# A two-layer encoder trunk: loads of the C values and of the bias rows put on GpSimd's queue, and a second buffer for loaded key rows

## The chip, the cores and the metric

The kernel runs on one core of one Trainium2 chip. The metric is the device time of one execution, in microseconds (us), smaller is better. A profiled execution has a span (first to last instruction) and a time of its own, which includes a little around the span.

## The reference, cut to what matters

The trunk has two layers over 2048 positions of width 1024, all in float32. In each layer a normalised input is projected into four groups of heads, each group does its own kind of attention, the four results are gated, concatenated, projected back and added to the input.

```python
for l in range(DEPTH):                                  # DEPTH = 2
    h = _rmsnorm(x, norm_g[l])
    z = jnp.einsum('bsd,de->bse', h, w_in[l])           # 1024 -> 3328 columns
    q_a, k_a, v_a, g_a, q_b, ..., g_d = jnp.split(z, offs, axis=-1)
    o_a = _dense_blocked(q_a, k_a, v_a, sc_hd)          # dense, 2048 keys for every query
    o_b = _window_sink(q_b, k_b, v_b, sink_b[l], sc_hd) # keys within 128 positions, sink logits
    o_c = _neighbourhood(q_c, k_c, v_c, rpb_c[l], sc_hd)
    o_d = _diff_blocked(q_d, k_d, v_d, lam, ...)        # difference of two softmaxes
    mix = concatenate([o_a * silu(g_a), o_b * silu(g_b), o_c * silu(g_c), o_d * silu(g_d)])
    x = x + jnp.einsum('bsm,md->bsd', mix, w_out[l])
return _rmsnorm(x, final_g)
```

Group C, which the change touches, sees the 2048 positions as a grid of 32 rows by 64 columns. Every query attends to a neighbourhood of 8 grid rows by 16 columns around it, and a learned bias by relative position is added to each logit:

```python
kg = jnp.take(k, idx, axis=1)...; vg = jnp.take(v, idx, axis=1)...   # 8 rows x 32 columns per block
sc = jnp.einsum('brcqhd,brclhd->brchql', qg, kg) * scale
sc = jnp.where(mask, sc + bias, NEG_INF)
p = jax.nn.softmax(sc, axis=-1)
o = jnp.einsum('brchql,brclhd->brcqhd', p, vg)
```

## The kernel before, in words

Each layer has three attention stages and an output projection. In the first stage the D columns of the input projection are computed for 16 tiles of 128 positions (`d_post`, `d_stack`). In the second, 32 units of D attention run while the rest of the input projection (A, B and C columns) is fed in between as filler; its results (q, k, v and gates of A, B and C) are stored to DRAM, the C values as `vc_d`, the C keys as `ksC`. The third stage, where the change lies, does the attention of A, B and C from those stored tensors. Then `out_proj` (L190) multiplies with `w_out`.

The third stage has two passes of 16 steps (the loop at L1117). In pass 0, step t does one unit of A (its first key head, 128 queries, 2048 keys) and two units of B. In pass 1, step t does one unit of A (second key head) and two units of C (two heads each); here a C tile is half of a band of 4 grid rows: `rg, ch = divmod(t, 2)`, band rg of eight, left or right half of the columns. One step issues scores on TensorE (S, Sb, Sc), max on VectorE (L497, L1001, L1037), exp on ScalarE, transposes of P (L513, L530) and their copies out of PSUM (L472, L474), and products with the values (L519 for A, L538 for B and C). At the end of a unit GpSimd multiplies the gate tile by the reciprocal of the softmax sum (`finish`, L543, tile gg, two buffers), TensorE transposes gg (`finish2`, L548), VectorE multiplies it with the output (L551, L558), and the product is stored to DRAM (mx, L552, L561).

What is loaded, and from where, in this stage:

- `k_batch` (L943): rows of stored keys (tile kl, 128 x 512 floats, pool "ql", L1068) come by a DMA of SyncE's queue (L947), are transposed on TensorE (kT, L98) and written into the key tiles. B and A need one kl for a batch, C two. Keys of C are made in pass 0, steps 12 to 15 (`prep`, L1098). Although the pool is named ql, only key rows live there; the queries (L963) have a pool of their own, qst.
- `load_vc` (L932): the values of C for a band, 9 or 12 grid rows by 40 columns for each half. Three grid rows of a half make one DMA (L940), 120 partitions of 1 KB, so 6 DMAs for the first and the last band and 8 for each other band, 60 in a layer. Destination is a slot of the pool "big" (10 slots).
- `load_bias` (L146): a tile of bias rows. GpSimd fills it with the mask value (L148), then four DMAs (L152), one for each grid row of the band, write 32 partitions by 4 heads by 320 floats each. The two inner tiles (bint, one for each half) serve bands 1 to 6; the tile of an edge band (bedge, one buffer, `cb`) is filled anew for each half of bands 0 and 7, so 6 bias tiles and 24 DMAs in a layer.
- `q_batch` (L959), `load_gate` (L608) and the stores of mx also issue from SyncE's queue.

The order of instructions on each queue is set by the framework when the kernel is built: the context is opened with `schedule_with_timeline_sim=True` (L1169). It plays the program through on a model of the engines and lets an instruction of later program order go ahead on its queue where the model finds the queue free and the operands and buffers ready. On the chip each queue then runs strictly in that fixed order, and an instruction that waits holds up all behind it. So a load written inside a C unit can stand many steps earlier on its queue, as soon as the model sees its buffer free.

Of the kernel before, what the change touches and what calls it, by code (L numbers as in the profile page):

```python
# [46 lines left out]
def c_window(rg):  # L47

    if rg == 0:
        return 0, 9  # L50
    if rg == 7:
        return 23, 9
    return 4 * rg - 4, 12
# [24 lines left out]
def trunk_kernel(ctx, tc, x, norm_g, w_in, w_out, qn_a, kn_a, sink_b, rpb_c, lam_q1, lam_k1, lam_q2, lam_k2,  # L78
                 subln_d, final_g, rope, bmask, out, depth=DEPTH):
    nc = tc.nc  # L80
# [65 lines left out]
    def load_bias(l, dst, rg, ch):  # L146
        w0, nr = c_window(rg)
        G.memset(dst, NEG)  # L148
        for r in range(4):
            i0 = min(max(4 * rg + r - 4, 0), 24) - w0  # L150
            row = w0 + i0 - 4 * rg - r + 7
            nc.sync.dma_start(out=dst[r * 32:r * 32 + 32, :, i0 * 40:i0 * 40 + 320],  # L152
                              in_=rep_d[l][ch][:, :, row * 40:row * 40 + 320])

    ht = {}
# [103 lines left out]
    for l in range(depth):  # L259
# [200 lines left out]
        with tc.tile_pool(name="sm", bufs=6, reuse_waits="tile") as sm, \  # L460
# [263 lines left out]
            with tc.tile_pool(name="st2", bufs=5, reuse_waits="tile") as st, tc.tile_pool(name="w2", bufs=10, reuse_waits="tile") as wp, \  # L724
# [175 lines left out]
                with tc.tile_pool(name="bb", bufs=1, reuse_waits="tile") as bbp, tc.tile_pool(name="p1", bufs=1, reuse_waits="tile") as p1p:  # L900
                    kds = {(0, 0): kd0[0], (0, 1): kd0[1]}

                    def get_kd(kv):
                        def f(c):
                            if (kv, c) not in kds:
# [7 lines left out]
                                  v=lambda h, j, kv=kv: vd[:, j, kv * 64:(kv + 1) * 64]) for kv in range(2) for t in range(NT)]  # L913
# [14 lines left out]
            def load_v(g):  # L928
                v = big2.tile([128, NT, 128], F32, tag="b", name=f"v{g}")
                nc.sync.dma_start(out=v, in_=vs_d[g])  # L930
                vt[g] = v

            def load_vc(rg):
                w0, nr = c_window(rg)
                v = big.tile([128, 2, 4, 256], F32, tag="b", name="vc")
                for ch in range(2):
                    for j in range(nr // 3):
                        k0 = (w0 + 3 * j) * 64 + 24 * ch
                        src = bass.AP(tensor=vc_d.tensor, offset=vc_d.offset + k0 * 256, ap=[[16384, 3], [256, 40], [1, 256]])
                        nc.sync.dma_start(out=v[0:120, ch, j, :], in_=src)  # L940
                return v

            def k_batch(ql, g, b):  # L943
                c = slice(b * 512, (b + 1) * 512)
                for pr in range(2 if g == "C" else 1):
                    kl = ql.tile([128, 4, 128], F32R, tag="kl", name="kl")
                    nc.sync.dma_start(out=kl.bitcast(F32), in_=ks_d[g, b][:, :, pr * 128:(pr + 1) * 128])  # L947
                    p = tps.tile([128, 512], F32, tag="t", name="kT")
                    for i in range(4):
                        transpose_raw(p[:, i * 128:(i + 1) * 128], kl[:, i, :])  # L950
                    if g != "A":
                        k0 = kt[g][2 * pr]
                        A.copy(k0[0:64, c], p[0:64, :])
                        V.tensor_tensor(k0[64:128, c], p[0:64, :], k0[0:64, c].bitcast(F32), op=ALU.subtract)
                    k1 = kt[g][2 * pr + 1]
                    A.copy(k1[64:128, c], p[64:128, :])
                    V.tensor_tensor(k1[0:64, c], p[64:128, :], k1[64:128, c].bitcast(F32), op=ALU.subtract)
# [94 lines left out]
            def a_unit(kv, t, q, pre):  # L1052
                return dict(kv=kv, t=t, s=a_scores, par=True, ev=EVA1 if kv else EV3, ns=8, nv=8, fin=fin_plain, fb=kv, q=q, pre=pre,
                            front=dense_front, back=dense_back, get_o=own_o, oc=0,
                            v=lambda h, j: vt["A"][:, j, kv * 64:(kv + 1) * 64])
# [8 lines left out]
            def small_unit(sc, i, t, q, px, fb, ns, nv, bias=None, pre=lambda: None):  # L1064
                return dict(kv=i, t=t, s=sc, par=False, ev=EVC if sc is c_scores else EVB, ns=ns, nv=nv, fin=fin_plain, fb=fb, q=q, pp=px, bias=bias, pre=pre,
                            front=small_front, back=small_back, get_o=pair_o, oc=128 * i, ptp=ptp)

            with tc.tile_pool(name="qst", bufs=2, reuse_waits="tile") as qst, tc.tile_pool(name="ql", bufs=1, reuse_waits="tile") as ql, \  # L1068
                    tc.tile_pool(name="cb", bufs=1, reuse_waits="tile") as cb, tc.tile_pool(name="px", bufs=4, reuse_waits="tile") as px, \
                    tc.tile_pool(name="pt", bufs=2, reuse_waits="tile") as ptp, \  # L1070
                    tc.tile_pool(name="ops2", bufs=1, space=PSUM, reuse_waits="tile") as ops2, \
                    tc.tile_pool(name="tps3", bufs=1, space=PSUM, reuse_waits="tile") as tps3:
                tpool = cycle([tps, tps, tps3])
                load_v("A")
                kt["B"] = [big.tile([128, S], F32R, tag="b", name=f"kB{i}") for i in range(2)]
                k_batch(ql, "B", 0)
                load_v("B")
                bint = [None, cb.tile([128, 4, 480], F32, name="bint1")]
                cc_ = {}
                cm = {"pool": cb}  # L1080
                qq = {}

                def prep(ps, t):
                    if t < NT:
                        g = "BC"[ps]
                        if ps == 0 and t % 4 == 2 and t < 14:
                            k_batch(ql, "B", t // 4 + 1)
                        if ps == 0 and t == 4:
                            kt["A"].append(big.tile([128, S], F32R, tag="b", name="kA1"))
                        if ps == 0 and 4 <= t < 8:  # L1090
                            k_batch(ql, "A", t - 4)
                        if ps == 1 and t == 2:
                            bint[0] = big2.tile([128, 4, 512], F32, tag="b", name="bint0")[:, :, 0:480]
                            load_bias(l, bint[0], 3, 0)
                        if ps == 0 and t == 8:
                            load_bias(l, bint[1], 3, 1)
                            kt["C"] = [big.tile([128, S], F32R, tag="b", name=f"kC{i}") for i in range(4)]
                        if ps == 0 and t >= 12:  # L1098
                            k_batch(ql, "C", t - 12)
                        qq["A", ps, t] = q_batch(qst, "A", t, 2 * ps, 2)  # L1100
                        qq[g, ps, t] = q_batch(qst, g, t, 0, 4)
                    elif ps == 0:
                        prep(1, 0)

                def get_bias(t, pr):
                    rg, ch = divmod(t, 2)
                    if ch == 0 and pr == 0:
                        cc_["v"] = load_vc(rg)
                    if rg not in (0, 7):
                        return bint[ch], cc_["v"]  # L1110
                    if pr == 0:
                        cc_["e"] = cb.tile([128, 4, 360], F32, tag="bedge", name="bedge")
                        load_bias(l, cc_["e"], rg, ch)
                    return cc_["e"], cc_["v"]
                prep(0, 0)
                units = []
                for ps in range(2):  # L1117
                    for t in range(NT):
                        units.append(a_unit(ps, t, lambda t=t, ps=ps: qq["A", ps, t], lambda t=t, ps=ps: prep(ps, t + 1)))
                        for i in range(2):  # L1120
                            if ps == 0:
                                units.append(small_unit(b_scores, i, t, lambda t=t: qq["B", 0, t], px, 2 + i, 2,
                                                        (min(t + 2, NT) - max(t - 1, 0) + 1) // 2))
                            else:
                                units.append(small_unit(c_scores, i, t, lambda t=t: qq["C", 1, t], px, 4 + i, 2, 2,
                                                        lambda t=t, i=i: get_bias(t, i)))
                                units[-1]["cm"] = cm
                def ex3(step):
                    if step == WOU:
                        for k in range(KD):  # L1130
                            if k == MS0:
                                ms_first.append(load_split(mx_d[0].rearrange("p a b -> p (a b)"), dv, "qd"))
                            wo_tiles.append(load_split(w_out[l, k * 128:(k + 1) * 128, :], dv, "qd"))
                drive([units[i:i + 3] for i in range(0, len(units), 3)], GAP3, iter(()), 0, ex3)
# [39 lines left out]
```

## Time and profile before

| what | value |
|---|---|
| median of 3 runs | 3717.33 us (3710.25 to 3719.14) |
| the profiled execution's own time | 3713.1 us |
| its span | 3711.3 us |
| mean granted TensorE clock in it | 0.978 of full speed |
| TensorE (PE) busy | 3516.1 us, 95% of the span |
| VectorE (DVE) busy | 2492.1 us, 67% |
| ScalarE (ACT) busy | 2095.2 us, 56% |
| GpSimd (POOL) busy | 944.4 us, 25% |
| third stage, about | 1081 to 1700 us (layer 0), 2945 to 3540 us (layer 1) |

Engines are named as in the profile: PE is the matmul side of TensorE, PEld its weight loads, DVE is VectorE, ACT ScalarE, POOL GpSimd, SP SyncE; SPq is SyncE's queue, whose rows are DMA issues. "L940" is line 940 of the kernel. In a timeline a row is: start, duration, engine, line, operation, output and inputs, count, and in brackets the idle time before it with the instruction that ended it. In a table of stretches a row is: the stretch, its length, then busy time (and count) of PE, PEld, DVE, ACT, POOL, then granted clock, DMA share and GB/s. In the list of waits a row is: who waited on whom, the total in us, how many times, the longest. In the chain of waits a row is: start, duration, and what the end of the program hung on at that time.

### The profile page before, as it was taken

Reading aid. Unit: us, or ns where it says so; the run is one execution under the profiler, and the core shown is the slowest. Engines: PE = TensorE matmul, PEld = TensorE weight load, DVE = VectorE, ACT = ScalarE, POOL = GpSimd, SP = SyncE. Lnnn points to the kernel's source line nnn. Section 1 sums busy time; section 2 is a strip of 40 time slices with the busy share of each in tenths; the row PEclk is TensorE's granted clock in tenths of the full one; section 3 lists DMA queues with packets and bytes.
Section 4 is the critical chain, followed back from the end, with each engine's and each line's share of the span. In section 5 each row is a group of like instructions: output and inputs, shape, how many; then the busy total and the mean of one; then the engine's idle time right before and its main releaser. Section 6 shows DMA issues by size and latency. Waiting matters only on the chain.

```text
span 3711.3 us, 71694 instructions
## 1 busy us (share of the span) xinstructions
PE 3516.1 (95%) x25232; PEld 2967.4 (80%) x25232; DVE 2492.1 (67%) x7829; ACT 2095.2 (56%) x3961; POOL 944.4 (25%) x1604
## 2 busy tenths in 40 slices
PE   8989999999989788999999899999999897899999
PEld 8979898888957666777899798989888676677787
DVE  4377878778777665774233778787877776667733
ACT  4345656556657565772143556565666676667721
POOL 4455324533100000001034553254321000000000
PEclk9999999999999998999999999999999899999999
DMA  4532225332133323325345323252232323343243
GB/s 142 191 100 83 80 76 172 86 83 83 59 98 86 89 83 107 93 78 181 132 129 192 98 78 86 78 182 73 78 84 73 90 81 92 88 117 89 87 151 119
DMA packets 353867, 386.44 MB, mean 104 GB/s; under 512 B 58914, under 2 KB 296674, under 8 KB 348386
## 3 DMA queue, kind: packets, MB, share of 16 engines
q1 hardware_dynamic: 349186, 366.11, 33.4%
q10 hardware_dynamic: 4320, 15.73, 1.2%
q8 instruction: 200, 3.28, 0.4%
q14 instruction: 161, 1.32, 0.1%
HBM read 258.83 MB, written 122.86 MB: 103 GB/s over the span
## 4 chain that ended last, share of the span: by engine, by line
PE 76%; DVE 7%; DMA 5%; POOL 4%; ACT 3%; issue 3%; SPq 2%; POOLq 0%; DVEq 0%; ACTq 0%
PE O L519 11%; PE S L496 10%; PE PTp L513 10%; PE y L222 10%; PE z L319 9%; PE z L321 9%; PE z L323 9%; DVE P L497 3%; PE PTp L530 2%; PE Obc L538 2%; ACT P L504 2%; PE Sc L1036 2%; SPq L940 1%; DMA wst<-in_w_in_dram 1%; DVE wt L313 1%
## 5 line engine op out<-in xcount | busy, mean ns | idle before, releaser
L497 DVE TENSOR_SCALAR_CACHE_REDUCE P<-S 128x512 f32<-128x512 f32 x1536 | 1017.7, 686 | 255.6 <-PE S L496 166.2
L319 PE MATMUL z<-wt,ht 128*128 128x256 f32 (+1 forms) x3008 | 891.3, 297 | 19.8 <-POOL wt L312 10.4
L321 PE MATMUL z<-wt,ht 128*128 128x256 f32 (+1 forms) x3008 | 882.9, 294 | 2.6 <-DVE wt L313 2.6
L323 PE MATMUL z<-wt,ht 128*128 128x256 f32 (+1 forms) x3008 | 882.3, 294 | 0.0
L513 PE MATMUL PTp<-idr,P 128*128 128x128 f32 x4096 | 624.6, 278 | 19.4 <-ACT P L474 10.3
L474 ACT COPY P<-PTp 128x512 f32<-128x512 f32 x864 | 491.3, 583 | 217.1 <-PE PTp L513 210.4
L319 PEld LDWEIGHTS z<-wt,ht 128*128 128x128 f32 x3008 | 568.8, 189 | 38.8 <-POOL wt L312 12.5
L504 ACT ACTIVATE P<-P,nm 128x2048 f32<-128x2048 f32 x256 | 513.9, 2008 | 144.4 <-DVE jk L503 139.9
L321 PEld LDWEIGHTS z<-wt,ht 128*128 128x128 f32 x3008 | 569.0, 189 | 16.1 <-DVE wt L313 4.6
L513 PEld LDWEIGHTS PTp<-idr,P 128*128 128x128 f32 x4096 | 491.5, 143 | 111.0 <-issue 23.6
L323 PEld LDWEIGHTS z<-wt,ht 128*128 128x128 f32 x3008 | 569.1, 189 | 8.4 <-issue 0.8
L496 PE MATMUL S<-kA,q 128*128 128x512 f32 x1024 | 348.1, 435 | 0.3
L543 POOL TENSOR_TENSOR gg<-gt,rzh 128x128 f32<-128x128 f32 x192 | 78.8, 411 | 1016.1 <-PE O L548 578.4
L222 PE MATMUL y<-wot,ms 128*128 128x512 f32 x1440 | 332.9, 393 | 3.4 <-ACT ms L211 2.0
L222 PEld LDWEIGHTS y<-wot,ms 128*128 128x128 f32 x1440 | 271.9, 189 | 64.2 <-ACT ms L211 2.4
L720 DVE SCALAR_TENSOR_TENSOR P<-P,cf,P 128x2048 f32<-128x2048 f32 x128 | 306.4, 2394 | 2.5
L312 POOL TENSOR_SCALAR wt<-wst,g 128x256 fp32r<-128x256 f32 (+1 forms) x336 | 208.2, 631 | 390.0 <-PE z L323 290.8
L504 ACT ACTIVATE P<-P,nm,rr_a 128x2048 f32<-128x2048 f32 x128 | 268.8, 2100 | 62.6 <-DVE jk L503 61.8
L519 PE MATMUL O<-P,vA 128*64 128x256 f32 x2048 | 272.6, 392 | 0.0
L519 PE MATMUL O<-P,vd 128*64 128x256 f32 x2048 | 240.9, 388 | 1.6 <-ACT P L474 1.6
L313 DVE SCALAR_TENSOR_TENSOR wt<-wst,g,wt 128x256 fp32r<-128x256 f32 (+1 forms) x344 | 195.3, 596 | 44.2 <-POOL wt L312 40.5
L496 PE MATMUL S<-kdt,qd 128*128 128x512 f32 x512 | 214.6, 442 | 8.3 <-DVE P L497 5.8
(195 smaller groups left out, 5130.6 us busy)
## 6 DMA issues: line engine op xcount, KB each, us to landing
wst<-in_w_in_dram SPq DMA_DIRECT2D x320, 128.0 KB
qd<-qd SPq DMA_DIRECT2D x128, 128.0 KB
htd<-ht SPq DMA_DIRECT2D x16, 1024.0 KB
ht<-htd SPq DMA_DIRECT2D x16, 1024.0 KB
q<-qsA SPq DMA_DIRECT2D x128, 128.0 KB
q<-qsB SPq DMA_DIRECT2D x64, 256.0 KB
q<-qc SPq DMA_DIRECT2D x64, 256.0 KB
mload<-mx ACTq DMA_DIRECT2D x30, 512.0 KB
```

What stands on the lines that cost most here:

```text
L222: PE.matmul(ys[c], lhsT=ms[:, a, kc], rhs=wts[k][:, b, c * 512:(c + 1) * 512], start=(k == 0 and i == 0), stop=(k == KD - 1 and i == 2))
L313: V.scalar_tensor_tensor(wt[:, 1, :], s, g8[:, k:k + 1], wt[:, 0, :].bitcast(F32), op0=ALU.mult, op1=ALU.subtract)
L319: PE.matmul(z, lhsT=h[:, 0, kc], rhs=wk[:, 0, :], start=(k == 0), stop=False)
L321: PE.matmul(z, lhsT=h[:, 0, kc], rhs=wk[:, 1, :], start=False, stop=False)
L323: PE.matmul(z, lhsT=h[:, 1, kc], rhs=wk[:, 0, :], start=False, stop=(k == KD - 1))
L474: A.copy(dst, src)
L496: PE.matmul(s, lhsT=q, rhs=k_ap[:, c:c + 512], start=(i == 0), stop=(i == len(q_list) - 1))
L497: V.tensor_scalar(p[:, c:c + 512], s, 1.0, None, op0=ALU.mult, op1=ALU.max, accum_out=mx[:, j:j + 1])
L504: A.activation(p, p, ACTF.Exp, bias=nm, scale=scale, accum_out=zacc)
L513: PE.transpose(tp[:, (h * 2 + a) * 128:(h * 2 + a + 1) * 128], p[:, h, j * 128:(j + 1) * 128], idn)
L519: PE.matmul(u["o"][a * 64:(a + 1) * 64, 0:256], lhsT=u["v"](0, j), rhs=u["p"][:, :, j * 128:(j + 1) * 128], start=(j >= NT - 2), stop=(j < 2))
L720: V.scalar_tensor_tensor(p0, p1, cf, p0, op0=ALU.mult, op1=ALU.add)
```

## The change

The 120 loads of C values (L940) and the 48 loads of bias rows (L152) are issued by GpSimd instead of SyncE, and the pool of the loaded key rows has two buffers instead of one. Nothing else is edited; the framework works out the order on all queues anew.

```diff
@@ load_bias @@
-            nc.sync.dma_start(out=dst[r * 32:r * 32 + 32, :, i0 * 40:i0 * 40 + 320],
+            nc.gpsimd.dma_start(out=dst[r * 32:r * 32 + 32, :, i0 * 40:i0 * 40 + 320],
                               in_=rep_d[l][ch][:, :, row * 40:row * 40 + 320])
@@ load_vc @@
-                        nc.sync.dma_start(out=v[0:120, ch, j, :], in_=src)
+                        nc.gpsimd.dma_start(out=v[0:120, ch, j, :], in_=src)
@@ the pools of the third stage @@
-            with tc.tile_pool(name="qst", bufs=2, reuse_waits="tile") as qst, tc.tile_pool(name="ql", bufs=1, reuse_waits="tile") as ql, \
+            with tc.tile_pool(name="qst", bufs=2, reuse_waits="tile") as qst, tc.tile_pool(name="ql", bufs=2, reuse_waits="tile") as ql, \
```

## The prediction

> **What bounds the kernel now.** I read the page first, then the chain of waits in the stretch where the page's PE slices dip, then the timelines of PE, SyncE's queue and GpSimd there.
>
> ```profile
> span 3711.3 us, 71694 instructions
> PE 3516.1 (95%) x25232; PEld 2967.4 (80%) x25232; DVE 2492.1 (67%) x7829; ACT 2095.2 (56%) x3961; POOL 944.4 (25%) x1604
> ```
>
> TensorE is busy 95% of the span, so all that a change of queues can win lies in the other 5%, 195 us, and in matmuls that run slowly after a pause. The edited lines belong to the third stage alone. There I cut the two layers into steps, from one transposed A gate (L548 into O) to the next: each row below is one step. The first and the fifth are undisturbed steps of pass 0 (with key rows of C) and of pass 1, the others are the long ones.
>
> ```profile
> 1261.68:1280.54 18.86, 17.96 (x141) 13.62 (x140) 15.13 (x55) 13.84 (x31) 1.20 (x3) 1.00 0.42 109
> 1280.54:1318.59 38.05, 19.57 (x136) 15.35 (x135) 15.41 (x54) 14.14 (x31) 1.20 (x3) 0.73 0.26 78
> 1372.03:1399.59 27.56, 18.62 (x118) 13.64 (x116) 12.46 (x39) 10.85 (x23) 4.14 (x5) 0.81 0.28 89
> 1399.59:1431.89 32.30, 18.70 (x127) 12.83 (x128) 11.73 (x47) 11.80 (x26) 2.49 (x4) 0.88 0.56 139
> 1484.83:1501.74 16.91, 16.91 (x142) 13.46 (x141) 12.44 (x46) 12.32 (x24) 1.20 (x3) 1.00 0.31 99
> 3126.47:3163.41 36.94, 18.82 (x136) 14.38 (x135) 15.33 (x54) 14.05 (x31) 1.20 (x3) 0.77 0.26 78
> 3216.56:3242.61 26.05, 17.93 (x118) 13.07 (x116) 12.10 (x39) 10.85 (x23) 4.16 (x5) 0.87 0.27 85
> 3242.61:3267.33 24.72, 18.66 (x128) 13.02 (x128) 12.79 (x46) 11.82 (x26) 2.49 (x4) 0.93 0.52 136
> ```
>
> An undisturbed step of pass 1 has PE busy for all of its 16.91 us: that is the floor, and moving loads cannot go under it. Six steps stand above their floor. Layer 0: 38.05 - 18.86 = 19.19, 27.56 - 16.91 = 10.65, 32.30 - 16.91 = 15.39. Layer 1: 36.94 - 18.86 = 18.08, 26.05 - 16.91 = 9.14, 24.72 - 16.91 = 7.81. The sum is **80.3 us**. It holds the pauses and the slow clock behind them (0.73 to 0.93 in those rows, 1.00 in the others). What PE waited for, layer 0 and then layer 1:
>
> ```profile
> PE kT L98 <- DMA kl<-ksC: 19.4, 3, 18.1
> PE Obc L538 <- DVE PT L472: 9.0, 2, 7.7
> PE O L548 <- ACT os L572: 8.5, 1, 8.5
> PE Sc L1036 <- DVE mxb L1037: 3.7, 1, 3.7
> ...
> PE kT L98 <- DMA kl<-ksC: 18.8, 3, 17.9
> PE Obc L538 <- DVE PT L472: 9.3, 2, 7.8
> PE Sc L1036 <- DVE mxb L1037: 4.4, 1, 4.4
> ```
>
> The first wait of each layer is the key rows of C. SyncE's queue says why: the load stood behind eleven loads of C values in a row. Its landing is in the chain of waits, and so is a later landing with nothing ahead of it.
>
> ```profile
> 1271.55 19.29 SPq L940 DMA_DIRECT2D vc<-vc  x11
> 1290.95 1.58 SPq L947 DMA_DIRECT2D kl<-ksC  x1
> ...
> 1290.95 8.41 DMA kl<-ksC
> ...
> 1316.89 3.00 DMA kl<-ksC
> ```
>
> The other waits come when pass 1 begins. VectorE and ScalarE stand still because a product could not be stored (mx), a bias tile had not come (bedge), and in layer 0 the next layer's sink logits (snk) were late. Each was issued between runs of C-value loads on the same queue, and each landed slowly:
>
> ```profile
> 1383.91 5.93 DMA mx<-mix
> ...
> 1401.11 10.69 DMA bedge<-rep
> ...
> 1422.85 6.16 DMA snk<-in_sink_b_dram
> ```
>
> **The change part by part: what leaves SyncE's queue.** Gone are 60 loads of C values and 24 of bias rows in each layer:
>
> ```profile
> L940 SPq DMA_DIRECT2D vc<-vc x120: 681/750/2484, 1266.4 to 3356.8; - x120
> L152 SPq DMA_DIRECT2D bedge<-rep x32: 538/597/1605, 1037.3 to 3493.9; - x32
> L152 SPq DMA_DIRECT2D bint<-rep x16: 538/568/634, 1033.8 to 3254.8; - x16
> ```
>
> By medians that is 60 x 0.75 + 16 x 0.60 + 8 x 0.57 = 59 us of queue time for a layer; in the long run it is 19.29 / 11 = 1.75 us a load. Of the two steps with 19.19 and 18.08 I count all but 1.5 us as gone: the key load is then issued at the end of the step's own short list, and the later landing of 3.00 us is what a single buffer still shows. The second key buffer works on the same stall from the other side, since a load may be issued while the tile before it is still being transposed; so either edit alone takes most of it, and together they earn it once. That is 37.3 - 1.5 = 35.8 us.
>
> Of the four steps at the start of pass 1 the excess is 10.65 + 15.39 + 9.14 + 7.81 = 43.0 us. Stores of mx, the sink logits, gates and queries stay on SyncE's queue and lose what stood before them. The bias tile does not: its fill and its four DMAs are now on one queue, GpSimd's.
>
> ```profile
> 1394.01 1.30 POOL L148 MEMSET bedge<- 128x1440 f32 x1 [16.16 <-DVE mxb L1037]
> ...
> 1399.52 4.03 SPq L152 DMA_DIRECT2D bedge<-rep  x4
> ```
>
> The fill waits until the tile's last reader is done; then 1.30 of fill, four issues and a landing must pass before the next half of the band can be scored. Before, that took 1411.8 - 1394.0 = 17.8 us; with four issues at 0.60 and a landing of 3 it is 1.3 + 2.4 + 3 = 6.7 us, less than a step, if no C-value load stands between. Some will, since 24 of a layer's 60 were issued between 1360.9 and 1421.4 us:
>
> ```profile
> L940 SPq DMA_DIRECT2D vc<-vc x24: 681/746/1754, 1360.9 to 1421.4; - x24
> ```
>
> I leave 4 us a layer for that, 8 in all, from bounds of 0 and of 11 (the tile no earlier than now, 17.8 - 6.7). That gives 43.0 - 8 = 35.0 us.
>
> **What GpSimd takes on.** The trace of before has no DMA issued from GpSimd, so the price of one there is unknown. The nearest rows are the same transfers from SyncE: 0.54 us below (a bias issue), 0.75 us (a C-value issue without a jam), 1.75 us above (in the jam). I take 0.75, the row of the same transfer; there is no reason for less than nothing. [...]
>
> Who waits behind such a load on GpSimd's queue? The gate products gg:
>
> ```profile
> 1485.18 0.40 POOL L543 TENSOR_TENSOR gg<-gt,rzh 128x128 f32<-128x128 f32 x1 [9.98 <-PE O L548]
> ...
> 1484.83 0.27 PE L548 MATMUL O<-idr,gg 128*128 128x128 f32 x1
> 1488.54 0.27 PE L548 MATMUL Obc<-idr,gg 128*128 128x128 f32 x1
> 1491.35 0.27 PE L548 MATMUL Obc<-idr,gg 128*128 128x128 f32 x1
> ```
>
> gg has two buffers: this one is written as soon as the transpose at 1484.83 frees its buffer, and transposed itself two transposes later, at 1491.35. So it may be late by 1491.35 - 1485.58 = 5.8 us before TensorE notices, and this is the tightest of the three in a step. A band's loads are 60 / 8 = 7.5 on average, 7.5 x 0.75 = 5.6 us if all stand in one piece ahead of it: within 5.8. GpSimd has the room too: 1.20 us busy in a step of 16.91. So the steady steps cost nothing at 0.75.
>
> At the start of the stage, eight bias loads are issued early and now fall between the last gates of D:
>
> ```profile
> 1033.81 2.56 SPq L152 DMA_DIRECT2D bint<-rep  x4
> ...
> 1037.31 2.48 SPq L152 DMA_DIRECT2D bedge<-rep  x4
> ...
> 1035.68 0.45 POOL L543 TENSOR_TENSOR gg<-gt,drs 128x128 f32<-128x128 f32 x1 [1.89 <-DVE drs L595]
> ```
>
> That gg ran as soon as its input drs came (1.89 us idle before it); a group of four loads of 2.5 us in front of it delays what follows by up to that, and there are two groups. I put 2 us for each layer, 4 in all, from 0 to 5.
>
> The sum: 35.8 + 35.0 - 4 = **66.8 us** less. The profiled execution took 3713.1 us, 1.8 more than its span; less 66.8 it would take 3646.3. The median of the three runs is 4.2 above the profiled one, so the forecast is 3717.3 - 66.8 = **3650.5 us**.
>
> **The rivals.** *The transfers stay in each other's way.* In the jam the loads went at 120 KB in 1.75 us, 69 GB/s, and the key rows landed 8.41 us after issue against 3.00. If that is a limit of the DMA engines and not of the queue, the late landings remain wherever they are issued from: 5.4 us for the key rows in each layer, 10.69 - 3 = 7.7 for bedge and 5.93 - 3 = 2.9 for mx in each, 6.16 - 3 = 3.2 for snk, in all 35.2; of the 80.3 there go 45.1, less the 1.5 and 4 of above: 39.6, which gives 3678. For it: the rate is flat through the run of eleven. Against: the DMA share is 0.26 in that step, so most engines had time. [...]
>
> *GpSimd's queue is the new wait (slower).* Place: gg behind a band's loads in the steady steps. If a load holds GpSimd for c us and each of the 16 bands' loads stands in one piece before the tight gg, TensorE loses 16 x (7.5c - 5.8). This eats the 66.8 at 7.5c = 10.0, c = 1.33 us. At the jammed 1.75 it is 16 x 7.3 = 117 us, so 50 slower: 3767. For it: nothing bounds c from above but the jam. Against: on SyncE the same burst was cut in two by short work, and five at 1.0 fit in 5.8.
>
> ```profile
> 1449.31 4.51 SPq L940 DMA_DIRECT2D vc<-vc  x5
> ...
> 1456.10 3.83 SPq L940 DMA_DIRECT2D vc<-vc  x3
> ```
>
> [...]
>
> *The place changes and the wait stays.* The order of all queues is worked out anew, and bias tiles behind C values on GpSimd could keep each bias tile 11 us late. With that (43.0 - 22 = 21), the D gates delayed by their 5 us a layer and c = 1.2 (16 x 3.2 = 51), the sum is 35.8 + 21 - 10 - 51 = -4: 3721, no change.
>
> **How the numbers follow.** The forecast's own case, with recoveries between 50 and 85, gets 0.62: the cause stands in the trace twice, in both layers, and the floor beside it. The transfers' rival gets 0.18, the place that changes 0.06, the slower one 0.14. A measurement of this kernel can tell about 0.3%, 11 us, from no change. Faster 0.80, the same 0.06, slower 0.14. The low end takes all 80.3 and the 7 us by which runs differ below the median: 3717 - 87 = 3630. The high end takes in the transfers' rival with the 8 us of bias left over and some of the spread: 3678 + 8 + 6 = 3692.
>
> **What would show it.** Right: the steps of 38.05 and 36.94 fall to about 19, those of 24.72 to 32.30 to 17 to 21, PE's wait for kl to under 4 us a layer, and the steady step stays at 16.91. The issue rows of vc on POOL show c; DMA landings of kl and bedge near 3 us speak against the transfers' rival, near 8 and 11 for it. Wrong: PE or PEld waiting for POOL gg, steady steps over 18, or a bias tile for band 0 that lands as late as now.

## The result, and the profile after

The changed kernel takes **3652.88 us** (median of 4 runs, 3651.88 to 3654.11); the kernel before, beside it, 3718.23 (3710.25 to 3726.55). The ratio is 0.9824, 95% interval 0.9802 to 0.9846. That is 65 us faster; the forecast was 3650.5, 67 us faster.

The profiled execution took 3653.0 us. The page of the changed kernel: TensorE is about as busy as before, GpSimd has 110 us more (the issues), the span is 60.0 us shorter.

```profile
span 3651.3 us, 71758 instructions
...
PE 3521.7 (96%) x25232; PEld 2959.9 (81%) x25232; DVE 2491.6 (68%) x7829; ACT 2094.8 (57%) x3961; POOL 1054.8 (29%) x1772
```

The same steps, cut in the same way (L548 to L548). In the table of stretches of the changed kernel the two key steps come first, then for each layer the four steps at the start of pass 1 as one stretch, then the four after them.

```profile
1290.65:1309.87 19.22, 18.34 (x136) 12.88 (x135) 15.13 (x54) 14.16 (x31) 1.20 (x3) 1.00 0.47 107
3094.84:3114.07 19.23, 18.35 (x137) 12.88 (x136) 15.13 (x54) 14.17 (x31) 1.20 (x3) 1.00 0.47 106
1348.41:1417.82 69.41, 65.45 (x488) 49.18 (x486) 47.11 (x181) 45.44 (x96) 32.35 (x51) 0.98 0.64 139
3152.61:3219.14 66.53, 64.62 (x487) 47.90 (x486) 45.91 (x180) 45.24 (x96) 32.64 (x52) 1.00 0.76 145
1417.82:1490.07 72.25, 72.25 (x556) 53.19 (x555) 50.39 (x179) 49.43 (x96) 16.76 (x30) 1.00 0.40 94
3219.14:3291.39 72.25, 72.25 (x555) 53.19 (x554) 50.39 (x179) 49.43 (x96) 16.14 (x30) 1.00 0.40 94
```

And the same two groups of four steps in the kernel before:

```profile
1357.60:1451.50 93.90, 71.36 (x487) 52.30 (x486) 48.68 (x181) 46.07 (x96) 9.03 (x15) 0.87 0.38 103
3202.16:3284.70 82.54, 68.36 (x487) 49.50 (x486) 48.71 (x180) 45.91 (x96) 9.05 (x15) 0.94 0.44 117
1451.50:1518.63 67.13, 67.13 (x556) 53.53 (x555) 49.30 (x180) 49.36 (x96) 4.80 (x12) 1.00 0.34 101
3284.70:3351.82 67.12, 67.12 (x555) 53.52 (x554) 49.29 (x179) 49.36 (x96) 4.80 (x12) 1.00 0.34 101
```

- Key steps: 38.05 to 19.22 and 36.94 to 19.23, **36.5 us** less.
- Start of pass 1: 93.90 to 69.41 and 82.54 to 66.53, **40.5 us** less. The clock is at 0.98 and 1.00 where it was 0.87 and 0.94: the pauses and the slow matmuls behind them went together.
- The next four steps: 67.13 to 72.25 and 67.12 to 72.25, **10.3 us** more, with TensorE busy all the time, at full clock, with the same number of matmuls. The forecast has no such term.
- All other steps of the stage: 3.1 less (the stage went from 578.5 to 538.7 and from 564.9 to 534.8 between its first and last gate). Ahead of the stage's first gate in layer 0: 11.1 us more, of which 5.4 lie in one interval of D's gates (below); the rest is spread over many intervals, and no run explains it. Between the two third stages 1.4 less, behind the second 0.1 more.

The sum, -36.5 - 40.5 + 10.3 - 3.1 + 11.1 - 1.4 + 0.1 = -60.0, is that of the spans.

In the list of waits of TensorE in layer 0's stage no wait for kl, for mx or for a bias tile is left among the large ones:

```profile
PE S L496 <- DVE P L497: 6.4, 7, 4.4
PE PTp L513 <- ACT P L474: 5.7, 5, 1.8
PE Obc L538 <- DVE ztb L1013: 4.0, 1, 4.0
```

The third of these comes from a late load that stayed: the sink logits, in the chain of the changed kernel, inside the one long step of layer 0 (24.76 us). It landed more slowly than before (6.16). In layer 1 a load of bias rows is in the chain:

```profile
1354.79 9.38 DMA snk<-in_sink_b_dram
...
3186.45 7.75 DMA bedge<-rep
```

The loads of bedge in the changed kernel, from issue to landing (us, min/median/max), lie between the 3 us and the 11 us that the prediction named as signs:

```profile
DMA to landing us min/median/max: 3.0/4.9/10.5
```

The price of an issue from GpSimd and the time to landing of the C values, from the rows of the tile vc in the changed kernel (ns for the issue, us to landing, each min/median/max):

```profile
L940 POOL DMA_DIRECT2D vc<-vc x120: 690/710/777, 1275.0 to 3294.2; - x120
...
DMA to landing us min/median/max: 4.8/6.4/12.4
```

A run of them holds GpSimd's queue no longer than that for each load, 6.34 / 9 = 0.70 us in its timeline, although they land slowly. Not all of them go out at once: 13 of the 120 issues stood behind the landing of an earlier load of C values, 11.1 us in all.

```profile
1275.03 6.34 POOL L940 DMA_DIRECT2D vc<-vc  x9
```

### The profile page after: what moved, and what is told of

It is laid out like the page before. It is cut to its first block, busy times and chain, and to the rows that moved or that the text cites. A ratio compares the mean times of both kernels' runs of the same rounds, so it can differ in the third digit from the quotient of the medians.

```text
span 3651.3 us, 71758 instructions
## 1 busy us (share of the span) xinstructions
PE 3521.7 (96%) x25232; PEld 2959.9 (81%) x25232; DVE 2491.6 (68%) x7829; ACT 2094.8 (57%) x3961; POOL 1054.8 (29%) x1772
## 4 chain that ended last, share of the span: by engine, by line
PE 70%; DVE 9%; POOL 3%; ACT 3%; issue 3%; DMA 3%; SPq 0%; POOLq 0%; DVEq 0%; ACTq 0%
PE O L519 11%; PE y L222 10%; PE S L496 9%; PE PTp L513 9%; PE z L319 7%; PE z L321 7%; PE z L323 7%; DVE P L497 4%; PE PTp L530 3%; PE Obc L538 3%; ACT P L504 2%; PE Sc L1036 2%; DVE wt L313 1%; DVE P L720 1%; POOL wt L312 1%
## 5 line engine op out<-in xcount | busy, mean ns | idle before, releaser
L319 PE MATMUL z<-wt,ht 128*128 128x256 f32 (+1 forms) x3008 | 892.1, 297 | 20.2 <-POOL wt L312 10.8
L519 PE MATMUL O<-P,vA 128*64 128x256 f32 x2048 | 278.5, 390 | 0.0
L519 PE MATMUL O<-P,vd 128*64 128x256 f32 x2048 | 242.8, 390 | 0.0
```

The source lines that it names most:

```text
L319: PE.matmul(z, lhsT=h[:, 0, kc], rhs=wk[:, 0, :], start=(k == 0), stop=False)
L519: PE.matmul(u["o"][a * 64:(a + 1) * 64, 0:256], lhsT=u["v"](0, j), rhs=u["p"][:, :, j * 128:(j + 1) * 128], start=(j >= NT - 2), stop=(j < 2))
```

## The experiments

Two theories stood against each other. **Queue**: SyncE's queue was too long, and taking 59 us of issues from it freed the loads behind. **Transfers**: the loads of C values themselves go slowly on the DMA engines, and the queue only showed it. Ratios are to the kernel before on the same chip, 3718 to 3724 us, each with its 95% interval.

**One part at a time.** Only the C values on GpSimd's queue:

```diff
-                        nc.sync.dma_start(out=v[0:120, ch, j, :], in_=src)
+                        nc.gpsimd.dma_start(out=v[0:120, ch, j, :], in_=src)
```

> Only the loads of C values go to GpSimd's queue; bias rows stay on SyncE's, one buffer for key rows. Queue theory (the stalls are time that SyncE's queue spends issuing C values): nearly the whole gain comes from this edit; both long key steps (38.05, 36.94) fall to 19 to 22 us, the four long steps at the start of pass 1 lose at least 35 of their 43 us of excess, time 3655 to 3668. Transfer theory (the C-value transfers hold the DMA engines wherever they are issued): the landings stay late, time about 3678. Buffer theory (the second key buffer earns the key steps): key steps stay above 30 us, time about 3690.

3662.72 us, 0.9838 (0.9824 to 0.9853). The key steps fall to 23.1 and 22.1 us; this part alone carries nearly all of the change. The steps of 18.3, 18.1, 17.5 and 18.3 after the start of pass 1 are here already.

TensorE's longest wait for kl in layer 0 falls from 18.1 to 4.0 us, though the load still lands slowly, in 6.36 us where it took 8.41. What changed more is that nothing stands ahead of it on SyncE's queue. So in the key steps the time on that queue was the larger part, and the slow landing the smaller. List of waits and chain of this kernel:

```profile
PE kT L98 <- DMA kl<-ksC: 5.2, 3, 4.0
...
1281.59 6.36 DMA kl<-ksC
```

Only the second buffer for key rows:

```diff
-... tc.tile_pool(name="ql", bufs=1, reuse_waits="tile") as ql, \
+... tc.tile_pool(name="ql", bufs=2, reuse_waits="tile") as ql, \
```

> Only the second buffer for key rows. Queue theory: the key load may be issued before the run of C values, so the key steps fall to about 19 and the start of pass 1 stays as long as before: 3718 - 36 = 3682. If the order still puts the load behind the run, nothing moves: 3718. Buffer theory: 3682, too, but then the kernel with both queue edits and one buffer keeps its long key steps.

3705.74 us, 0.9953 (0.9936 to 0.9970). The key steps are still 32.9 and 34.2 us. The wait for kl is gone from the list, and something else is late in its place:

```profile
PE PTp L530 <- DVE P L472: 13.0, 3, 12.2
```

The timeline of SyncE's queue in this kernel shows the run of eleven loads as it was, at 19.26 / 11 = 1.75 us each, ahead of key rows, gates and a store of mx:

```profile
1273.04 19.26 SPq L940 DMA_DIRECT2D vc<-vc  x11
1292.42 3.53 SPq L947 DMA_DIRECT2D kl<-ksC  x2
1296.37 1.04 SPq L616 DMA_DIRECT2D gt<-gsA  x1
1297.53 0.35 SPq L552 DMA_DIRECT2D mx<-mix  x1
```

So the second buffer cures one victim of the jam, not the jam.

C values and bias rows on GpSimd's queue, one key buffer (both `nc.gpsimd` edits of the diff above):

> Both queue edits, one buffer for key rows. Queue theory: the second buffer earns only the short waits for the second key tile of a batch, 0.6 us on PE and some more on what follows: 3653 to 3662, key steps 19 to 21 us. Buffer theory: key steps stay above 30, time about 3690.

3669.2 us, 0.9855 (0.9840 to 0.9870), beside 0.9838 for the C values alone: the bias rows add nothing.

C values on GpSimd's queue and two key buffers, bias rows left on SyncE's:

> C values on GpSimd's queue and two key buffers, bias rows back on SyncE's queue. Queue theory: the eight early bias loads no longer stand before the last D gates, which gives back the 5.4 us that layer 0 lost there, and SyncE's queue is free enough for the bias rows: 3645 to 3653. If the bias rows' place matters at the start of pass 1: above 3656, with bedge landing late again.

3647.83 us, 0.9793 (0.9777 to 0.9809): a little under the changed kernel's 0.9824. Moving the bias rows won nothing; if anything it cost.

**Does GpSimd's queue have slack?** The changed kernel with twice as many loads of C values, each with half of every row:

```diff
+                        for e in range(2):
...
+                            nc.gpsimd.dma_start(out=v[0:120, ch, j, 128 * e:128 * e + 128], in_=src)
```

> The changed kernel, but each load of C values is cut into two of half the floats (120 partitions of 512 bytes), so a band puts 16 issues on GpSimd's queue where it put 8. At the 0.70 us that an issue takes there a burst is 11.2 us. If a burst stands before a gate product that may be 5.8 us late, TensorE loses up to 5.4 us a band, 16 bands: up to 86 us, so up to 3739, and TensorE or its weight loads wait for POOL gg. If the gate products behind a burst have the 12 us that the first such step of the changed kernel shows: 3653 to 3660.

3651.25 us, 0.9813 (0.9798 to 0.9827): no slower, with 120 more issues at 0.72 us. In the third stage TensorE still waits for no gg. The slower rival lacked its price, and it lacked its place too.

**The late sink logits.** C values on GpSimd, two key buffers, and a tile of sink logits for each layer, so that they can be loaded early:

```diff
-        snk = lay.tile([128, 4], F32, tag="snk", name="snk")
+        snk = lay.tile([128, 4], F32, tag=f"snk{l}", name="snk")
```

> C values on GpSimd's queue, two key buffers, bias rows on SyncE's queue, and tiles of their own in each layer for the sink logits and their negatives, so that layer 1's load of them need not wait for layer 0's last reader. If that load, 9.4 us in landing with VectorE waiting for it, is what makes the step of 24.6 us in layer 0 longer than its twin of 19.2 in layer 1: 5 us less than with the one pair of tiles, about 3642. If VectorE would have waited for something else there: 3648.

3648.81 us, 0.9803 (0.9785 to 0.9822), not to be told from 3647.83. The step of 24.6 us is 19.2 now and the stage 4 us shorter in that trace, but it does not show in the time.

**Another queue.** The kernel of 3647.83 with the C values on ScalarE's queue instead of GpSimd's:

```diff
-                        nc.gpsimd.dma_start(out=v[0:120, ch, j, :], in_=src)
+                        nc.scalar.dma_start(out=v[0:120, ch, j, :], in_=src)
```

> Two key buffers, bias rows on SyncE's queue, and the C values issued from ScalarE's queue instead of GpSimd's. Queue theory: SyncE's queue is as free as with GpSimd, so the key steps fall to about 19, but ScalarE stands 0.75 to 1.75 us for each load between its exps and copies: 120 x 0.75 = 90 us of it, of which TensorE sees a part, 3660 to 3720. Transfer theory: runs of these loads take 1.75 us an issue there, too, and ScalarE is held up to 19 us at a time: above 3720.

3724.55 us, 1.0009 (1.0000 to 1.0019). SyncE's queue was relieved just as much, and in the key step of layer 0 TensorE waits for kl no more, yet all of the gain is gone. The jam went along with the loads: four in a row take 6.85 / 4 = 1.71 us each, ScalarE stands idle for 8 us behind them, and TensorE waits for ScalarE's copy. Timeline of ScalarE and list of TensorE's waits in this kernel:

```profile
1280.59 6.85 ACTq L940 DMA_DIRECT2D vc<-vc  x4
1287.48 0.37 ACT L474 COPY PT<-PTp 128x256 f32<-128x256 f32 x1 [8.01 <-issue]
...
PE Obc L538 <- ACT PT L474: 7.3, 1, 7.3
```

So the jam belongs to these loads and not to SyncE's queue. That a shorter SyncE queue is worth nothing does not follow, because here ScalarE's own work is held up in its place. The DMA view of that kernel in 1280:1288 us (queue, packets, MB, share of 16 engines) shows how the jam looks from the engines' side:

```profile
q10 hardware_dynamic: 533, 0.53, 20.2%
```

The kernel before in the middle of its jam, 1278:1290 us:

```profile
DMA packets 804, 0.82 MB, mean 68 GB/s; under 512 B 18, under 2 KB 803, under 8 KB 803
...
q1 hardware_dynamic: 803, 0.80, 20.2%
```

On both queues a fifth of the DMA engines' time and 67 to 68 GB/s, level. Three engines of 16 would be 18.75%. And three is the outermost count of the load's source, `[[16384, 3], [256, 40], [1, 256]]`: three grid rows of 40 positions. From GpSimd the same loads had a larger share of the engines. The changed kernel in 1274:1290 us, GpSimd's queue:

```profile
q0 software_dynamic: 2094, 1.42, 52.9%
```

The rate rose less than the share: 1.42 MB in 16 us is 89 GB/s.

That a load with three outer rows works on three engines only is the author's reading of these two shares, 20.2% and 20.2%; which engines they were the profile does not say. The next two kernels give the loads 40 and 120 outer rows.

**The shape, without any move.** The kernel before, each load of C values cut into its three grid rows of 40 positions, all on SyncE's queue, one key buffer:

```diff
-                        src = bass.AP(..., ap=[[16384, 3], [256, 40], [1, 256]])
-                        nc.sync.dma_start(out=v[0:120, ch, j, :], in_=src)
+                        for r in range(3):
+                            src = bass.AP(..., offset=... + (k0 + 64 * r) * 256, ap=[[256, 40], [1, 256]])
+                            nc.sync.dma_start(out=v[40 * r:40 * r + 40, ch, j, :], in_=src)
```

> The kernel before, but each load of C values is cut into three of one grid row each (40 partitions of 1 KB), all still on SyncE's queue: 180 issues in a layer instead of 60. Queue theory (what counts is the number of issues and their time on SyncE's queue): 180 issues of 0.3 to 0.5 us take 54 to 90 us of the queue instead of 45, so the key steps stay above 30 us and the time is 3718 or more. Transfer theory (a three-row load is confined to few DMA engines, which is what makes an issue take 1.75 us in a run): the jam goes, an issue in a run costs what a lone one does, eleven loads take 33 x 0.4 = 13 us instead of 19.3, key steps fall by 5 us or more each and the time to about 3695.

**3631.48 us**, 0.9759 (0.9742 to 0.9775): faster than the change by 0.0065 of the time, 24 us, with three times as many loads on the queue that was thought too long. SyncE's timeline: 18 short loads, six of the old ones, in 7.57 us, 1.26 for each old one, and the key load behind them.

```profile
1271.22 7.57 SPq L941 DMA_DIRECT2D vc<-vc  x18
1278.90 0.56 SPq L948 DMA_DIRECT2D kl<-ksC  x1
```

This left two readings, shape or size of a load. So the kernel before with one load as ever, 120 partitions of 1 KB, but from 120 successive positions:

```diff
-ap=[[16384, 3], [256, 40], [1, 256]]
+ap=[[256, 120], [1, 256]]
```

> The kernel before with one edit: a load of C values reads 120 successive positions instead of 40 positions from each of 3 grid rows. Bytes, partitions, queue (SyncE), number of loads and the order on TensorE, ScalarE and GpSimd are those of before; the values that come are others, so the output is not the reference's. If the jam is the shape of the load (three outer rows put it on few DMA engines, 120 KB in 1.75 us), it goes although nothing left the queue: the load issues in about 0.75 us in a long run, the key steps take 19 to 21 us, the time is 3625 to 3645 us, as with loads cut by grid rows (3631). If SyncE's queue itself is the limit (that many rows of 1 KB for one queue), the loads still take 1.75 us in a row, the steps stay at 37 to 38 us and the time at 3721.

This is an experiment and no kernel to use, since group C gets values of other positions.

3632.01 us, 0.9760 (0.9746 to 0.9773). Number, size and queue of the loads are those of before, and so is the order on ScalarE and GpSimd, and on TensorE but for a few swapped matmuls; only the shape differs. Here the 120 rows also follow each other without a gap in DRAM; the cut loads above read the same rows as before, with gaps, and won as much. **The cause of the jam is the shape.** The timeline of SyncE's queue, ten loads in a row at 0.48 us where eleven took 19.29:

```profile
1274.02 4.83 SPq L940 DMA_DIRECT2D vc<-vc  x10
```

The DMA view of the same kernel in 1274:1279 us shows a share five times the 20.2% of before:

```profile
q1 hardware_dynamic: 1216, 1.26, 100.8%
```

And in its chain the neighbours that had landed late, key rows (8.41 before), sink logits (6.16) and mx (5.93):

```profile
1281.76 3.46 DMA kl<-ksC
...
1366.27 3.08 DMA snk<-in_sink_b_dram
1374.62 3.02 DMA mx<-mix
```

**On top of the cut.** Cut loads on SyncE's queue, and two key buffers:

> The kernel before with each load of C values cut into three of 40 partitions, all on SyncE's queue, and two buffers for key rows. If the shape was the cause and is cured by the cut, the second buffer has left only the 1.4 and 0.9 us by which the key steps stand above 18.9, and the order of the queues is made anew: 3625 to 3635 us, the same as the cut alone. If it works as it did beside GpSimd's loads (3662.7 to 3647.8 us), 15 us go: 3617.

**3623.17 us**, 0.9741 (0.9728 to 0.9754), the fastest kernel of all here, 0.8% under the changed one. Its key steps are as short as the changed kernel's, and both groups of four steps at the start of pass 1 take 62.26 us (1339.12 to 1401.38 and 3131.03 to 3193.29), where the changed kernel has 69.41 and 66.53. Its table of stretches, the two key steps and two of the four steps at the start of pass 1:

```profile
1281.37:1300.61 19.24, 18.35 (x137) 12.90 (x136) 15.15 (x54) 14.18 (x31) 1.21 (x3) 1.00 0.48 133
3073.29:3092.52 19.23, 18.35 (x136) 12.89 (x135) 15.13 (x54) 14.16 (x31) 1.20 (x3) 1.00 0.46 131
1353.53:1368.28 14.75, 14.75 (x117) 11.69 (x116) 11.46 (x39) 11.32 (x23) 4.20 (x5) 1.00 0.51 137
1368.28:1384.71 16.43, 16.41 (x128) 12.46 (x127) 13.54 (x50) 11.77 (x25) 2.50 (x4) 1.00 0.71 171
```

The changed kernel with cut loads, on GpSimd's queue:

> The changed kernel with each load of C values cut into three of 40 partitions, on GpSimd's queue. If three outer rows slow the transfers there too, the landings of C values fall from 6.4 us (median) to about 3 to 4 and the late sink logits of layer 0 with them (the step of 24.8 us falls by 4 to 6), the 10 us of the new order and 5 of the gates of D stay: 3642 to 3648 us. If GpSimd's descriptors were spread over the engines anyway, landings stay near 6 and the time at 3652. If three short loads hold GpSimd longer than one (3 x 0.4 against 0.71 us) and gg comes late, 3655 to 3690.

3649.86 us, 0.9808 (0.9794 to 0.9821). The rows of vc: landings fall from 6.4 to 2.5 us (median), each with a third of the bytes. The last of three is issued 1.03 us after the first, so by these medians a whole old load is in after some 3.5 us (an estimate) against 6.4: the shape seems to slow them on GpSimd too. But three short loads hold its queue for 1.54 us where one took 0.71, and the time is the changed kernel's within the intervals.

```profile
L941 POOL DMA_DIRECT2D vc<-vc x360: 512/514/593, 1273.3 to 3305.2; - x180
...
DMA to landing us min/median/max: 1.8/2.5/5.4
```

The last kernel is the fastest one with the bias rows alone on GpSimd's queue:

> Against the version with cut loads of C values on SyncE's queue and two key buffers (0.9741 of before): the bias rows alone go to GpSimd's queue. If the two groups of four loads between the last gates of D cost what they did in the changed kernel (5.4 us in layer 0, nothing in layer 1) and a bias tile in pass 1 is as quick by either queue, 3628 us, ratio 0.9755. If the bias rows carry most of the 26 us between that version and the one with all these loads on GpSimd's queue, 3640 to 3649, ratio 0.979 to 0.981. If moving them costs nothing, 0.974.

Ratio 0.9772 (0.9758 to 0.9786) against 0.9741, that is 0.0031 x 3718 = 11.5 us slower. The same difference separates the changed kernel (0.9824) from the one with its bias rows on SyncE (0.9793), though there the intervals overlap. GpSimd's timeline just before layer 0's third stage shows the part that can be placed: between D's sums and the gate product stand eight issues, 4.59 us.

```profile
1033.89 0.70 POOL L118 TENSOR_TENSOR drs<-dme,epst 128x2 f32<-128x2 f32 x1 [2.15 <-DVE dme L116]
1034.53 2.41 POOL L152 DMA_DIRECT2D bint<-rep  x4
1036.93 2.18 POOL L152 DMA_DIRECT2D bedge<-rep  x4
1039.12 0.41 POOL L543 TENSOR_TENSOR gg<-gt,drs 128x128 f32<-128x128 f32 x1
```

The interval between the two D outputs there is 32.1 to 32.2 us in every kernel with bias rows on GpSimd, and 26.7 to 26.8 in the others. In layer 1 no interval grew so. Besides these 5.4 us, some 4 are in the two third stages (529.7 and 527.8 against 526.9 and 526.5), and the rest lies where no edited line is; what it comes from stays open.

## Why the prediction was right, point by point

- **Where the time was.** In six steps around the key loads and the start of pass 1: right. How much it was: too low, because the floor was. 16.91 us is a step with 142 matmuls, and the step of 27.56 that it was subtracted from has 118. In that place the fastest kernel has a step of 14.75 us, and its four steps at the start of pass 1 take 93.90 - 62.26 = 31.6 and 82.54 - 62.26 = 20.3 us less than before, where the prediction saw 43.0 in both layers together. Its gain, 0.0259 x 3718 = 96 us, is above the 80.3.
- **The key steps**, -35.8 forecast, -36.5 measured: right. But "either edit alone takes most of it" holds for the C values only (23.1 and 22.1 us); the second buffer alone left 32.9 and 34.2, because gates and a store of mx stood behind the same jam.
- **The start of pass 1**, -35.0 forecast, -40.5 measured. The low floor hid some of what could be won, and the 8 us left for late bias tiles were too much. What did stay is 7.1 and 4.3 us against the 62.26 of the fastest kernel. TensorE is idle for only 4.0 and 1.9 us of it (69.41 - 65.45 and 66.53 - 64.62); the 4.0 are the wait for the sink logits, so late bias tiles can have cost 1.9 at most. The rest is TensorE being busy for longer with the same matmuls. The steps one by one did not fall to 17 to 21 us as foreseen: work moved between them (24.76, 13.50, 13.00 and 18.16 in layer 0), so that only the groups of four can be compared.
- **The gates of D**, +4 forecast, 2 in each layer: +5.4 in layer 0, nothing to be seen in layer 1. Both groups of four issues came ahead of one gate, so they added up.
- **The price on GpSimd's queue**, 0.75 us taken, 0.71 measured, never above 0.78 in the changed kernel. The 1.0 and 1.2 that the rivals reckon with are assumed values that no run shows; five loads at 0.71 are 3.6 us. gg behind a whole band of loads was no wait of TensorE; the doubled loads confirm the slack.
- **"So the steady steps cost nothing": wrong in what it covers.** Two groups of four steps cost 10.3 us more, with three of the four over the 18 us that the prediction named as a sign of being wrong. gg is not the reason, since TensorE waits for nothing in them. The framework's new order is: in one such step of the changed kernel TensorE's half-width products (128*64, L519) stand in five pieces of 12, 4, 4, 6 and 6, before in two of 16. By the grouped lines of the first of these stretches, after and then before, the same 128 matmuls take 18.6 us instead of 15.6, which is 3.0 of the 5.1 us, and the other groups grow a little too:

```profile
L519 PE MATMUL O<-P,vA 128*64 128x256 f32 x128 | 18.6, 391 | 0.0
```

```profile
L519 PE MATMUL O<-P,vA 128*64 128x256 f32 x128 | 15.6, 385 | 0.0
```

  The longer steps came wherever whole loads of C values went to GpSimd (18.3, 18.1, 17.5 and 18.3 us also with the C values alone), and not with the flat loads, whose order on TensorE is nearly that of before (16.4, 16.9, 16.9 and 16.9). That the pieces are the reason is read from these rows; no run shows it by itself.
- **The sum**, -66.8 forecast, is -65.4 by the medians and -60.1 by the two profiled executions (3713.1 and 3653.0); the runs of before spread over 16 us. That it came so near is partly luck. The 10.3 of the longer steps were missed, and so were 7.1 ahead of layer 0's third stage, beyond the 4 that were counted. Against them stand 5.5 more at the start of pass 1, 0.7 in the key steps, 3.1 in other steps and 1.3 elsewhere, and the last 5 lie in the choice of before: its median, 3718.23, is that much above its profiled execution.
- **The reason was right as far as it went, and stopped short.** That the key load stood behind the run of C values is borne out: the wait for kl of 18.1 us ended with the landing at 1290.95 + 8.41 = 1299.4, so it began at 1281.3, and 9.7 us of it were over before the load was issued; with the C values on GpSimd as the only edit, the wait for kl in layer 0 fell by 14.1 us, to 4.0, and a faster landing (6.36 us against 8.41) gave only 2.1 of that. Why the run took 1.75 us a load was not asked. The argument against the transfers' rival was that the DMA share was 0.26, "so most engines had time". They had; the loads did not use them, and the level 68 GB/s went with a share of 20.2%, near the 18.75% of three engines (the author's estimate; no run counts them). With another shape on the same queue both halves of the stall go, the time on the queue and the slow landing (3.46 us). GpSimd's queue helps because a run of these loads holds it for 0.70 us each, where it holds SyncE's for 1.75 and ScalarE's for 1.71; how much the larger share of the engines adds no run separates. The rival had the cause right and the price wrong: it took the slow landings as costing the same wherever the loads are issued from. They stayed in part, for the C values (6.4 us), the sink logits (9.38), the bias rows (median 4.9) and, with one buffer, the key rows (6.36), but they cost TensorE little.
- **The time to issue** was not small here: eleven issues held SyncE's queue for 19.29 us, and from GpSimd the C values alone gave 0.9838. The ScalarE run (1.0009) moved the held time to another engine and saved none.

## What to carry to other kernels

When a run of equal loads on one queue goes at a level rate well below what the DMA engines move elsewhere, look at the shape of the load before its queue. Here, on one queue, three outermost entries went with 20.2% of the engines' time and 68 GB/s, 120 of them with 100.8% and 253 GB/s. Try a long count outermost, or cut the load; here that won 2.4% in a few edited lines, and the move to another queue, with a second buffer, 1.8%. A change of queues also makes the order on all engines anew, so compare undisturbed steps too, not only those that were to get faster.

## What the runs showed of the hardware

- 120 KB in 120 rows of 1 KB: 1.75 us a load in a run with the outer counts 3 and 40, 0.48 us with 120; 68 against 253 GB/s, on the same queue. Between other issues one load with three outer rows held the queue for 0.70 us (at 1268.55 in the kernel before), and the median of all 120 is 0.75: the 1.75 showed only within a run of them.
- Loads issued behind a run of slow ones landed late: key rows took 8.41 us behind eleven of them and 3.46 behind ten loads of as many bytes each in the other shape. An engine's own work waited behind such a run on its queue, too: ScalarE stood idle for 8.01 us behind four of them.
- An issue from GpSimd took 0.71 us for 120 rows, 0.51 for 40 and 0.55 for a bias load, with little spread (0.69 to 0.78 for the 120 rows in the changed kernel). From SyncE, in a run, a short load took 7.57 / 18 = 0.42 us and a flat one of 120 rows 0.48.
